# An FFN on split fp32 weights: high parts first, wide casts, and one early feature group of three blocks by seven products

## The chip, the cores and the metric

The kernel runs on one core of a Trainium2 chip. The metric is the device time of one launch in microseconds. Five queues work side by side: TensorE (PE in the profile; its weight loads are PEld), VectorE (DVE), ScalarE (ACT), GpSimd (POOL) and SyncE (SP), which here issues nearly all DMAs. Weights (about 300 MB of fp32) stream from HBM once.

## The reference

One transformer layer on 256 latent tokens of 2048 features, with 256 context tokens that serve as keys and values only. The second half, which the change touches, is an adaLN-modulated SwiGLU FFN of 5632 hidden features:

```python
def swiglu(u, w_gate, w_up, w_down):
    return (jax.nn.silu(u @ w_gate) * (u @ w_up)) @ w_down
...
x = layer_norm(DN_ALPHA * x + g1 * (heads @ w_out[layer]), ln1_g[layer], ln1_b[layer])

x = layer_norm(DN_ALPHA * x + g2 * swiglu(modulate(x, sh2, sc2), w_gate[layer], w_up[layer], w_down[layer]),
               ln2_g[layer], ln2_b[layer])
```

`sh2`, `sc2` and `g2` are columns of `silu(c) @ w_ada + b_ada`, one row each.

## The kernel before

**Split products.** Each fp32 operand is split into a high part, a cast to fp32r on ScalarE, and a low part, the difference on VectorE. A product is three matmuls of 128x128 by 128x512 (`mm3`, L340): high x high, high tokens x low weights, low tokens x high weights, in this order for each chunk of 128 features. A weight load brings 4 chunks x 512 columns (1 MB, `load_raw`) into one of four raw buffers; `split_raw` (L320) cuts it into two pieces of 1024 columns, each with its own cast (L331) and difference (L332), in one of four slots of `hi` and `lo`. Such a step ("a plain step", `project`, L1494) makes 4 chunks x 2 token halves x 3 = 24 matmuls.

**Stages.** Up to about 390 us an order searched by a planner (`Flow`) runs modulation, q/k/v, attention and the output projection; its steps take slots of `hi` and `lo` as the pool gives them. The FFN that follows is written as lists of steps, and the framework's scheduler sets the order on each queue from that. Gate and up have 11 blocks of 512 hidden features; the 2048 input features are four groups of four chunks.

- *Early projections* (about 390 to 582 us). Features of groups 2 and 3 need `sh2` and `sc2`, which are still being summed from `w_ada`: VectorE multiplies and adds 1024 columns at a time (`vector_sum`, L466), 32 times for two groups, then turns the row into columns (`folded_columns`, L1150) with a few matmuls. Meanwhile TensorE works on the groups that are ready: group 0 for blocks 0 to 2, groups 0 and 1 for blocks 3 to 9 (`first_half`, L1655), with results copied by ScalarE to `spills` in SBUF. `merge` (L290) spreads the ada steps evenly between the projection steps (L1713). The last two projections run after the last features are there.
- *Late gate and up* (about 582 to 878 us). Block pairs (f0, f0 + 1): group 2 of the gate goes through `folded` (L1541), Winograd's form of Strassen's scheme: with two token halves, two halves of four chunks and two column blocks, seven products take the place of eight. VectorE forms differences of weights and (once) of tokens for it, ScalarE copies partial sums from bank to bank. Plain steps of up run between the products. Then gating, a transpose through DRAM (`flip_steps`, L1610) and the split of the hidden features (`place`).
- *Down* (about 878 to 1110 us). `down_step` for four column blocks, with group `FOLD_H` again folded, the sums for `g2` beside it, and the last normalisation at the end.

PSUM has four `acc` and four `wk` banks. SyncE issues loads in order, so a load that waits for a raw buffer holds those behind it.

Of the kernel before, what the change touches and what calls it, by code (L numbers as in the profile page):

```python
# [13 lines left out]
F32 = mybir.dt.float32  # L14
# [9 lines left out]
P = 128  # L24
# [26 lines left out]
FOLD_K = 8  # L51
FOLD_H = 6
# [19 lines left out]
class Flow:  # L72
# [194 lines left out]
def dit_layer(ctx: ExitStack, tc: tile.TileContext, x, c, cx, c_ctx, w_ada, b_ada, w_in, q_norm_g,  # L267
# [8 lines left out]
    whl = ctx.enter_context(tc.tile_pool(name="whl", bufs=HL_BUFS))  # L276
# [17 lines left out]

    def fill(pool, nbytes):

        pool.tile([P, nbytes // 4], F32, tag="fill", name="fill")
# [5 lines left out]
    stats = main.tile([P, NT, 4, 6], F32, tag="stats", name="stats")  # L303

# [12 lines left out]
    def load_split(w, k0, c0, nk=G4, width=NB, spare=False):  # L317
        return split_raw(load_raw(w, k0, nk, c0, width), spare)

    def split_raw(raw, spare=False):  # L320

        parts = []
        for s in range(0, raw.shape[-1], SUB * NB):
            n = min(SUB * NB, raw.shape[-1] - s)
# [3 lines left out]
            else:  # L328
                hi = whl.tile([P, SUB * NB], F32R, tag="hi", name="hi")
                lo = whl.tile([P, SUB * NB], F32R, tag="lo", name="lo")  # L330
            nc.scalar.copy(hi[:, :n], raw[:, s : s + n])  # L331
            nc.vector.tensor_tensor(lo[:, :n], raw[:, s : s + n], hi[:, :n].bitcast(F32), op=ALU.subtract)  # L332
            parts += [(hi[:, j : j + NB], lo[:, j : j + NB]) for j in range(0, n, NB)]
        return parts
# [138 lines left out]
    def split_rows(sb, dst, s):  # L473
        hi = whl.tile([P, SUB * NB], F32R, tag="hi", name="hi")[:, :NB]
        lo = whl.tile([P, SUB * NB], F32R, tag="lo", name="lo")[:, :NB]
# [112 lines left out]
    def flow_weights(w, k0, nk, c0, width=NB, where=("raw", "araw"), spare=False, small=False, behind=(None, None)):  # L588
# [3 lines left out]
        for s in range(0, nk * width, SUB * NB):  # L592
# [4 lines left out]
            def cast(hl=hl, s=s, n=n):  # L597
                if spare:
                    hl.hi, hl.lo = (b4([P, SUB * NB], F32R, c) for c in ("hi", "lo"))
                else:  # L600
                    hl.hi = whl.tile([P, SUB * NB], F32R, tag="hi", name="hi")
                    hl.lo = whl.tile([P, SUB * NB], F32R, tag="lo", name="lo")
# [547 lines left out]
    def folded_columns(sb, n):  # L1150
# [7 lines left out]
        ps = wk_bank()  # L1158
        for q in range(4):
            nc.tensor.matmul(ps[32 * q : 32 * q + 32, :n], lhsT=grp[0], rhs=rv[:, q], start=True, stop=True)  # L1160
        return ps

    def second_modulation(g, sums):
        def done(sb):
            ps = folded_columns(sb, 8)
# [820 lines left out]
```

## Time and profile before

| | us |
|---|---|
| time, median of 3 runs (lowest to highest) | 1122.85 (1122.63 to 1124.99) |
| span of the profiled execution | 1121.0 |
| first FFN matmul | 390.4 |
| last matmul ends about | 1110 |
| granted TensorE clock, mean | 0.996 |

The span runs from the first to the last instruction of one profiled execution; no time of that execution beside its span is recorded, and the runs' median lies 1.85 us above it. In the timeline each matmul of 512 columns lasts 0.39 us, yet consecutive ones overlap: what counts is the distance from start to start. In the groups, a row has busy time, the mean length of one in ns, then the idle time of the engine just before and what ended it.

### The profile page before, as it was taken

To read this page: it belongs to the slowest core of one execution; us is meant where nothing else is said; L and a number is where in the kernel's file an instruction comes from. 1 tells how busy PE (TensorE), PEld (TensorE's weight loads), DVE (VectorE), ACT (ScalarE), POOL (GpSimd) and SP (SyncE) were. 2 spreads that over 40 slices of the span, in tenths; PEclk is the share of its full clock that TensorE was granted. 3 is DMA by queue.
4 is the path that set the end of the run, shared out by engine and by line. 5 is a ranking of instruction groups with operands and counts; after the bars stand their busy time and mean duration, and the time that the engine had idled before them with its cause. 6 is when DMAs were issued, how large, how long until landed. Compare 5 with 4: busy or idle time off the path is not lost.

```text
span 1121.0 us, 14130 instructions
## 1 busy us (share of the span) xinstructions
PE 1102.3 (98%) x5213; PEld 883.7 (79%) x5213; DVE 903.4 (81%) x1133; ACT 598.7 (53%) x875; POOL 36.7 (3%) x82
## 2 busy tenths in 40 slices
PE   8999999999999999999999999999999999999995
PEld 6766688777887788888888878888888888888884
DVE  5763589899999888787778697988996987689876
ACT  3341554878685356444475565767766344444442
POOL 1000030110100001000000000000000000000000
PEclk9999999999999999999999999999999999999998
DMA  9999999778999778999956677777776998669742
GB/s 321 394 385 375 393 362 377 247 234 274 345 332 395 249 269 321 348 318 296 336 182 216 223 220 266 234 246 271 228 267 216 329 348 293 228 235 379 287 149 76
DMA packets 178317, 321.26 MB, mean 287 GB/s; under 512 B 8732, under 2 KB 43196, under 8 KB 175943
## 3 DMA queue, kind: packets, MB, share of 16 engines
q1 hardware_dynamic: 177528, 320.03, 81.7%
q8 instruction: 41, 0.67, 0.2%
q10 hardware_dynamic: 720, 0.33, 0.1%
q14 instruction: 28, 0.23, 0.1%
HBM read 304.07 MB, written 16.25 MB: 286 GB/s over the span
## 4 chain that ended last, share of the span: by engine, by line
PE 91%; DMA 3%; DVE 2%; ACT 1%; SPq 1%; issue 0%; ACTq 0%; DVEq 0%
PE acc L341 20%; PE acc L343 20%; PE acc L342 20%; PE wk L342 8%; PE wk L341 8%; PE wk L343 8%; PE wk L1081 2%; PE wk L654 2%; DMA raw<-in_w_in_dram 2%; DVE lo L332 1%; DMA lgb<-in_ln_g_dram 1%; PE wk L755 1%; SPq L569 1%; DMA xt<-in_x_dram 0%; PE wk L1414 0%
## 5 line engine op out<-in xcount | busy, mean ns | idle before, releaser
L331 ACT CAST hi<-raw 128x1024 fp32r<-128x1024 f32 x279 | 290.7, 1054 | 256.4 <-PE acc L343 162.4
L332 DVE TENSOR_TENSOR lo<-raw,hi 128x1024 fp32r<-128x1024 f32 x279 | 336.1, 1220 | 103.6 <-ACT hi L331 101.4
L341 PE MATMUL acc<-hi,u2h 128*128 128x512 f32 x390 | 152.5, 391 | 0.0
L343 PE MATMUL acc<-hi,u2l 128*128 128x512 f32 x390 | 151.7, 390 | 0.7 <-DVE u2l L1669 0.7
L342 PE MATMUL acc<-lo,u2h 128*128 128x512 f32 x390 | 151.8, 389 | 0.0
L603 ACT CAST hi<-raw 128x1024 fp32r<-128x1024 f32 (+1 forms) x86 | 87.4, 1030 | 113.8 <-DMA raw<-in_w_in_dram 63.2
L466 DVE SCALAR_TENSOR_TENSOR adav<-raw,cs,adav 128x512 f32<-128x512 f32 (+1 forms) x128 | 121.4, 949 | 8.4 <-DMA raw<-in_w_ada_dram 4.9
L606 DVE TENSOR_TENSOR lo<-raw,hi 128x1024 fp32r<-128x1024 f32 (+1 forms) x86 | 101.3, 1194 | 16.3 <-ACT hi L603 15.5
L341 PE MATMUL acc<-hi,uh 128*128 128x512 f32 x256 | 103.7, 405 | 1.3 <-ACT uh L769 0.8
L342 PE MATMUL wk<-lo,u2h 128*128 128x512 f32 x264 | 103.1, 390 | 0.5 <-DVE lo L332 0.5
L343 PE MATMUL wk<-hi,u2l 128*128 128x512 f32 x264 | 102.7, 389 | 0.0
L341 PE MATMUL wk<-hi,u2h 128*128 128x512 f32 x264 | 102.2, 389 | 0.0
L342 PE MATMUL acc<-lo,uh 128*128 128x512 f32 x256 | 100.5, 392 | 0.6 <-DVE lo L606 0.6
L343 PE MATMUL acc<-hi,ul 128*128 128x512 f32 x256 | 100.1, 391 | 0.4 <-DVE ul L784 0.4
L341 PE MATMUL acc<-hi,hTh 128*128 128x512 f32 x236 | 92.0, 390 | 0.4 <-ACT acc L1901 0.4
L342 PE MATMUL acc<-lo,hTh 128*128 128x512 f32 x236 | 91.8, 389 | 0.0
L343 PE MATMUL acc<-hi,hTl 128*128 128x512 f32 x236 | 91.8, 389 | 0.0
L343 PEld LDWEIGHTS acc<-hi,u2l 128*128 128x128 f32 x390 | 73.2, 188 | 16.2 <-DVE u2l L1669 1.1
L341 PEld LDWEIGHTS acc<-hi,u2h 128*128 128x128 f32 x390 | 73.2, 188 | 16.1 <-ACT u2h L1668 0.8
L342 PEld LDWEIGHTS acc<-lo,u2h 128*128 128x128 f32 x390 | 73.2, 188 | 15.1
L341 PEld LDWEIGHTS acc<-hi,uh 128*128 128x128 f32 x256 | 48.1, 188 | 19.0 <-issue 5.6
L342 PEld LDWEIGHTS wk<-lo,u2h 128*128 128x128 f32 x264 | 49.5, 188 | 12.0 <-DVE lo L332 1.8
(277 smaller groups left out, 1748.0 us busy)
## 6 DMA issues: line engine op xcount, KB each, us to landing
raw<-in_w_ada_dram SPq DMA_DIRECT2D x70, 1024.0 KB, 7.7
raw<-in_w_gate_dram SPq DMA_DIRECT2D x44, 1024.0 KB, 6.7
raw<-in_w_up_dram SPq DMA_DIRECT2D x44, 1024.0 KB, 5.6
raw<-in_w_down_dram SPq DMA_DIRECT2D x44, 1024.0 KB, 5.8
raw<-in_w_ada_dram SPq DMA_DIRECT2D x48, 512.0 KB, 5.9
raw<-in_w_in_dram SPq DMA_DIRECT2D x18, 1024.0 KB, 11.0
raw<-in_w_out_dram SPq DMA_DIRECT2D x16, 1024.0 KB, 6.5
pd<-hx SPq DMA_DIRECT2D x64, 128.0 KB, 3.4
```

Of the source, the lines that this page charges most:

```text
L331: nc.scalar.copy(hi[:, :n], raw[:, s : s + n])
L332: nc.vector.tensor_tensor(lo[:, :n], raw[:, s : s + n], hi[:, :n].bitcast(F32), op=ALU.subtract)
L341: nc.tensor.matmul(ps, lhsT=xh, rhs=w[0], start=first, stop=False, skip_group_check=seeded)
L342: nc.tensor.matmul(ps, lhsT=xh, rhs=w[1], start=False, stop=False, skip_group_check=seeded)
L343: nc.tensor.matmul(ps, lhsT=xl, rhs=w[0], start=False, stop=last, skip_group_check=seeded)
L466: nc.vector.scalar_tensor_tensor(a[:, c : c + piece], raw[:, f : f + piece], cs[:, 4 * (g * (G4 * NB // w) + j) + 2, None], a[:, c : c + p ...
L569: nc.sync.dma_start(room.t, w[k0 * P : (k0 + 1) * P, c0 : c0 + width])
L603: nc.scalar.copy(hl.hi[:, :n], raw.t[:, s : s + n])
L606: nc.vector.tensor_tensor(hl.lo[:, :n], raw.t[:, s : s + n], hl.hi[:, :n].bitcast(F32), op=ALU.subtract)
L654: nc.tensor.matmul(bank.t[32 * j : 32 * j + 32, :width], lhsT=cs[:, 4 * k + 2 - 2 * i : 4 * k + 34 - 2 * i], rhs=raw.t[:, c * width : (c + ...
L755: nc.tensor.transpose(ps.t[:, (j * 2 + t) * P : (j * 2 + t + 1) * P], src, ident)
L1081: nc.tensor.matmul(o_ps.t[:, : 2 * P].rearrange("p (g q) -> p g q", q=32), lhsT=v, rhs=pv[:, k], start=k == 0, stop=k == 3)
```

## The change

1. *Seven products early.* `EARLY_F = (4, 6, 8)`: group 1 (features 512 to 1023, `FOLD_E = 4`) of these blocks no longer takes a plain step each for gate and up. `folded` runs with the gate columns and the up columns of the same block as its pair, after token forms made once (`token_forms(*heads, ...)`). Its five stages stand between plain steps of other blocks; then group 0 of up and of gate is added onto the same banks, and the results go to `spills` (up by VectorE additions, gate by ScalarE copies). The gate weights land in two tiles of their own (`halves_of`), the up weights in a raw buffer.
2. *High parts first.* `products` issues, for all chunks and token halves of a step, the two matmuls on the high weights, then those on the low weights. The attention part, the first FFN products and the tail keep `mm3`.
3. *Wide casts.* `hi` and `lo` are one tile each with four slots of 1024 columns, given in turn (`part_pair`); a plain step's 2048 columns are cast and subtracted by one instruction each, in two neighbouring slots, the first of them even. The last steps (`fine=True`) keep pieces of 1024. The planner's part takes the slot that its own schedule shows free first.
4. *Smaller ones.* The ada steps are spread by a count of VectorE work (`spread`); the matmuls behind `folded_columns` are a step of their own; some VectorE operations of the late stage go over both token halves at once; the `g2` sums run over 1024 columns.

```diff
-        for s, s.start, pools in self.search()[0]:
+        best = self.search()[0]
+        free = [(0.0, i) for i in range(self.room["hl"])]
+        left = {b: b.left for s, _, _ in best for b in s.give}
+        for s, s.start, pools in best:
             for b, b.pool in zip(s.take, pools):
-                pass
+                if b.pool == "hl":
+                    free.sort()
+                    b.slot = free.pop(0)[1]
...
+    def spread(steps, extra, load):
+
+        loads = [load.get(s, (24, 2)) for s in steps]
+        share = (sum(v for _, v in loads) + 2 * len(extra)) / sum(n for n, _ in loads)
+        res, extra, debt = [], list(extra), 0.0
+        for s, (n, v) in zip(steps, loads):
+            res.append(s)
+            debt += n * share - v
+            while extra and debt > 0:
+                res.append(extra.pop(0))
+                debt -= 2
+        return res + extra
...
+    def part_pair(n):
+
+
+        wide = SUB * NB
+        if n > wide:
+            turns[0] += turns[0] % 2
+        i = turns[0] % HL_BUFS
+        turns[0] += -(-n // wide)
+        return [parts[c].rearrange("p b n -> p (b n)")[:, i * wide : i * wide + n] for c in ("hi", "lo")]
...
+    def split_raw(raw, spare=False, fine=False):
+
+        n = raw.shape[-1]
+        cols = []
+        for s in range(0, n, SUB * NB if spare or fine else n):
+            m = SUB * NB if spare or fine else n
...
+                hi, lo = part_pair(m)
+            split(hi, lo, raw[:, s : s + m])
+            cols += [(hi[:, j : j + NB], lo[:, j : j + NB]) for j in range(0, m, NB)]
+        return cols
...
+    def products(banks, w, first, last, seeded=False):
+
+
+        for j, x in enumerate(banks):
+            for i, (ps, xs) in enumerate(x):
+                for h in xs:
+                    nc.tensor.matmul(ps, lhsT=h, rhs=w[j][0], start=first and not seeded and j == 0 and h is xs[0], stop=False,
+                                     skip_group_check=seeded)
+        for j, x in enumerate(banks):
+            for ps, xs in x:
+                nc.tensor.matmul(ps, lhsT=xs[0], rhs=w[j][1], start=False, stop=last and j == len(banks) - 1,
+                                 skip_group_check=seeded)
...
+    def halves_of(w, k0, c0):
+
+        res = []
+        for i, c in enumerate("hl"):
+            half = halves0.pop(0) if halves0 else pb.tile([P, 2 * NB], F32, tag=f"hT{c}0", name="half")
...
-    def folded(columns, forms, shared):
+    def folded(columns, forms, shared, first=wk_bank):
...
+        def product(ps, m, piece, first):
+            products([[(ps, forms[m][j])] for j in range(2)], split_raw(piece), first, True, not first)
...
+    def fold_steps(f):
...
+        def shared(e):
+            nc.scalar.copy(up[:, 0, :], e)
+
+        def stage(i):
+            if i == 0:
+                st["it"] = folded([(w, FOLD_E, f * NB) for w in (w_gate, w_up)], early, shared, acc_bank)
+            st["banks"] = next(st["it"])
+
+        def own(i, w):
+            project(st["banks"][i], w, f, 0, None, 3, True)
+            for t in reversed(range(NT)):
+                if i:
+                    nc.vector.tensor_add(up[:, t, :], up[:, 0, :], st["banks"][i][t])
+                else:
+                    nc.scalar.copy(gate[:, t, :], st["banks"][i][t])
...
+        steps = fold_steps(f)
+        load.update(zip(steps, ((6, 2), (6, 3), (12, 3), (12, 2), (6, 1), (24, 3), (24, 2))))
+        normal = [s for e in range(f) if e not in EARLY_F for s in firsts_of[e]]
+        at = len(normal) - 2
+        rest, AT_F = first_half[at:], at
+        mixed = []
+        for s in steps[:4]:
+            mixed += [s, rest.pop(0)]
...
-    run(merge(first_half[2 * ONE_F + 1 : cutoff], side))
+    run(spread(first_half[2 * ONE_F + 1 : cutoff], side, load))
```

More of the change, by code (lines that the diff above doesn't have):

```diff
@@ L51 @@
 FOLD_K = 8
+FOLD_E = 4
+EARLY_F = (4, 6, 8,)
 FOLD_H = 6
@@ L600, in cast @@
                 else:
[L601 to L602 removed]
+                    hl.hi, hl.lo = (parts[c][:, hl.slot, :] for c in ("hi", "lo"))
                 nc.scalar.copy(hl.hi[:, :n], raw.t[:, s : s + n])
@@ L1157, in folded_columns, with sums, place @@
         rv = r[:, : 4 * n].rearrange("p (c q) -> p q c", q=4)
[L1158 to L1161, printed above, removed]
+        def sums():
+            ps = wk_bank()
+            for q in range(4):
+                nc.tensor.matmul(ps[32 * q : 32 * q + 32, :n], lhsT=grp[0], rhs=rv[:, q], start=True, stop=True)
+            return ps
+        return sums
     def second_modulation(g, sums):
+        st = {}
         def done(sb):
-            ps = folded_columns(sb, 8)
+            st["sums"] = folded_columns(sb, 8)
+        def place():
+            ps = st["sums"]()
             ks = slice(g * 4, g * 4 + 4)
@@ L1169, in done @@
             combine(g)
-        return ada_vector_steps((3 * D + g * NB, 4 * D + g * NB), NB, sums, done)
+        return ada_vector_steps((3 * D + g * NB, 4 * D + g * NB), NB, sums, done) + [place]
     def flow_vector(starts, width, a, span):
@@ L1558, in folded @@
         yield
-        products(e, 1, b11, True)
+        product(e, 1, b11, True)
         tt(b12, b22, b12, op=ALU.subtract)
@@ L1562, in folded @@
         yield
-        products(b, 2, b11, False)
+        product(b, 2, b11, False)
         c = acc_bank()
@@ L1630, in places @@
         def places():
-            for t in range(NT):
-                place(f, t, hf[t])
+            place(f, wide)
             if f == FOLD_H:
@@ L1648, in step @@
                 if g == 0:
-                    st["accs"] = [acc_bank() for _ in range(NT)]
+                    st["accs"] = [acc_bank() if f < ONE_F else wk_bank() for _ in range(NT)]
                 project(st["accs"], w_, f, g, 0, groups[f] * 4 - 1)
@@ L1653, in step @@
                         nc.scalar.copy(spills[f][i][:, t, :], st["accs"][t])
-            first_half += [lambda g=g, step=step: step(g) for g in range(groups[f])]
+            firsts_of[f] += [lambda g=g, step=step: step(g) for g in range(groups[f])]
+    def fold_steps(f):
+        st = {}
+        gate, up = spills[f]
+        def shared(e):
[11 more added lines that the diff above has]
+                    nc.scalar.copy(gate[:, t, :], st["banks"][i][t])
+        return [lambda i=i: stage(i) for i in range(5)] + [lambda: own(1, w_up), lambda: own(0, w_gate)]
+    first_half, load = [], {}
+    for f in range(SPLIT_F):
+        if f not in EARLY_F:
+            first_half += firsts_of[f]
+    AT_F = 0
+    for f in reversed(EARLY_F):
+        steps = fold_steps(f)
[6 more added lines that the diff above has]
+            mixed += [s, rest.pop(0)]
+        if f + 1 < SPLIT_F and len(rest) > 2:
+            first_half[at:] = mixed + [steps[4]] + steps[5:] + rest
+        else:
+            first_half[at:] = mixed + steps[4:] + rest
     late_sums = [lambda: vector_sums(2 * NB), lambda: pb.tile([P, 2 * NB], F32, tag="lgb", name="adav")]
```

148 lines of the change are left out of this document (76 added, 72 removed).

## The prediction

> **What bounds the kernel now.** I read the page first (shares, chain of waits), then windows over the FFN, then single matmuls in the timeline.
>
> ```profile
> span 1121.0 us, 14130 instructions
> ...
> PE 1102.3 (98%) x5213; PEld 883.7 (79%) x5213; DVE 903.4 (81%) x1133; ACT 598.7 (53%) x875; POOL 36.7 (3%) x82
> ...
> PE 91%; DMA 3%; DVE 2%; ACT 1%; SPq 1%; issue 0%; ACTq 0%; DVEq 0%
> ```
>
> TensorE is busy 98% of the span and makes 91% of the chain that ended last. A busy PE need not be at its pace, so the timeline is needed: two rows of one unbroken run of projections, the first and the last of 123.
>
> ```profile
> 469.78 0.39 PE L341 MATMUL acc<-hi,u2h 128*128 128x512 f32 x1
> ...
> 497.43 0.39 PE L343 MATMUL acc<-hi,u2l 128*128 128x512 f32 x1
> ```
>
> (497.43 − 469.78) / 122 = 0.2266 us from start to start. That is the price of one matmul wherever nothing is late. [...]
>
> The windows show what the other engines do meanwhile: first the stretch the change rewrites (early projections, 434 to 571 us), then the late gate and up stage.
>
> ```profile
> 434.00:571.00 137.00, 137.00 (x627) 112.98 (x626) 100.45 (x92) 68.19 (x81) 1.64 (x7) 1.00 0.92 314
> ```
> ```profile
> 571.00:878.00 307.00, 306.46 (x1350) 252.80 (x1350) 259.84 (x289) 193.56 (x244) 0.00 (x0) 1.00 0.72 237
> ```
>
> Columns after the width are PE, PEld, DVE, ACT, POOL, then clock, DMA share and GB/s. In the early stretch PE never idles, DVE is busy 100.45 of 137 us (73%), DMA has a share of 0.92. Late, DVE is at 259.84 / 307 = 85%. So TensorE's count of matmuls sets the FFN's time, and VectorE is next. Where VectorE was late it shows as three places in the late stage:
>
> ```profile
> 645.77 0.39 PE L341 MATMUL wk<-hi,u2h 128*128 128x512 f32 x1
> 646.32 0.50 PE L342 MATMUL wk<-lo,u2h 128*128 128x512 f32 x1 [0.17 <-DVE lo L332]
> ...
> 653.04 0.39 PE L341 MATMUL wk<-hi,u2h 128*128 128x512 f32 x1
> 653.80 0.50 PE L342 MATMUL wk<-lo,u2h 128*128 128x512 f32 x1 [0.37 <-DVE lo L332]
> 654.14 0.40 PE L343 MATMUL wk<-hi,u2l 128*128 128x512 f32 x1
> ```
> ```profile
> 668.66 0.39 PE L341 MATMUL wk<-hi,u2h 128*128 128x512 f32 x1
> 669.01 0.50 PE L342 MATMUL wk<-lo,u2h 128*128 128x512 f32 x1
> 669.35 0.39 PE L343 MATMUL wk<-hi,u2l 128*128 128x512 f32 x1
> ```
> ```profile
> 636.00:670.00 34.00, 33.46 (x145) 26.79 (x144) 32.02 (x38) 19.90 (x26) 0.00 (x0) 1.00 0.61 192
> ```
>
> The low part of a weight piece arrived late. The steps are 0.55, 0.76 and 0.35 us instead of 0.23 (0.32 + 0.53 + 0.12 lost), and the step behind each is 0.34 instead of 0.23: together 1.3 us.
>
> **The change, part by part.** *Seven products.* A block's group 1 (features 512 to 1023) costs gate and up 2 x 24 = 48 matmuls; seven products of 6 cost 42. Three blocks: 18 matmuls x 0.2266 = **4.1 us** less on TensorE. Everything else of the fold lies on ScalarE, VectorE and DMA and costs only what makes a matmul late. The prices there:
>
> ```profile
> L332 DVE TENSOR_TENSOR lo<-raw,hi 128x1024 fp32r<-128x1024 f32 x49 | 59.7, 1220 | 29.4 <-ACT hi L331 29.3
> L466 DVE SCALAR_TENSOR_TENSOR adav<-raw,cs,adav 128x1024 f32<-128x1024 f32 x29 | 37.2, 1282 | 3.3 <-DMA raw<-in_w_ada_dram 3.2
> L1155 DVE STREAM_TRANSPOSE flip<-adav 128x512 f32<-128x512 f32 x4 | 2.8, 707 | 0.1
> L1156 DVE TENSOR_REDUCE fold<-flip 128x16 f32<-128x512 f32 x4 | 2.7, 676 | 0.0
> ```
> ```profile
> L1560 DVE TENSOR_TENSOR raw<-raw 128x1024 f32<-128x1024 f32 x7 | 8.4, 1203 | 0.0
> L1891 DVE TENSOR_TENSOR raw<-raw,room 128x2048 f32<-128x2048 f32 x3 | 6.9, 2287 | 0.1
> L1753 DVE TENSOR_TENSOR spill<-spill,wk 128x512 f32<-128x512 f32 x4 | 2.6, 680 | 0.0
> ```
> ```profile
> 517.29 1.28 DVE L466 SCALAR_TENSOR_TENSOR adav<-raw,cs,adav 128x1024 f32<-128x1024 f32 x1
> 518.49 1.22 DVE L332 TENSOR_TENSOR lo<-raw,hi 128x1024 fp32r<-128x1024 f32 x1
> 519.62 1.28 DVE L466 SCALAR_TENSOR_TENSOR adav<-raw,cs,adav 128x1024 f32<-128x1024 f32 x1
> ```
>
> Back to back a sum takes 1.20 us and a low part 1.13 us from start to start, 0.08 to 0.09 less than they last. The new order runs from the second gate step of block 3 to the gate step that ends block 8. TensorE: 24 + 3 x (42 products + 4 x 24 plain steps between them + 2 x 24 for group 0) = 582 matmuls = 131.9 us (600 and 136.0 before). VectorE in the same steps, back to back: 19 whole low parts x 2.20 (2.287 − 0.09) = 41.8; 21 product pieces x 1.13 = 23.7; 12 weight differences x 1.13 = 13.6; 6 additions of up x 0.60 = 3.6; the token forms about 2.6 (six operations of 256 or 512 columns); 32 sums x 1.20 = 38.4; their columns 4 x 0.65 + 4 x 0.60 = 5.0. Sum **128.7 us**; with the isolated durations (2.287, 1.220, 1.203, 0.680, 1.282) it is 138. So VectorE goes from 73% to 98% of the stretch. If it still waits 3.2 us for ada weights, as now, it stands at 131.9, exactly TensorE's time. The loss this brings is shown by no row of the stretch; bounds: 0 (the low part is asked for later, next item) and 138 + 3.2 − 131.9 = 9.3 us, less some 3 us by which VectorE can lag at the ends (an estimate: about half of a step of 24 x 0.2266 at each), so 6. Nearest is the window above with VectorE at 32.02 of 34 us (94%): 1.3 us lost, which over 132 us would be 5. There the low part was wanted by the second matmul; now most plain steps give it 16. I take **2 us**.
>
> *High parts first.* `products` issues a step's high matmuls (16 of 24) and then the 8 low ones: the low part is due 16 x 0.2266 = 3.6 us after the step begins, not 0.23. In a single product it is 4 of 6, 0.9 us. The same number of matmuls, the same number of weight loads. All three delays above are under 0.9 us, so I take them as gone: **−1.3 us** (bounds 0 and −1.3). Nothing else in the FFN waits for a low part for long, so no more is to be had.
>
> *Wide casts.* Each pair of 1024-column casts and differences becomes one of 2048.
>
> ```profile
> L331 ACT CAST hi<-raw 128x1024 fp32r<-128x1024 f32 x49 | 51.6, 1054 | 54.8 <-PE acc L343 52.3 <-DMA raw<-in_w_up_dram 1.3 <-DVE adav L466 1.2
> L1653 ACT COPY spill<-acc 128x512 f32<-128x512 f32 x26 | 15.3, 589 | 14.0 <-PE acc L343 12.8
> ...
> L1480 ACT CAST u2h<-uf 128x512 fp32r<-128x512 f32 x2 | 1.2, 622 | 0.0
> ```
>
> ScalarE now waits for slots, 52.3 us of it on TensorE, so what it saves is idle time and counts nothing; on VectorE a pair costs 2.287 instead of 2.44, already in the sum. But a wide cast needs two of four slots free at once, and starts the step's first matmul only when all 2048 columns are done: some 1054 + 1024 x 0.84 = 1.9 us, 0.84 being (1054 − 622 of a 512 cast) / 512. With one-slot products between plain steps, an odd slot is skipped and the plain step always returns to the same two. Then its cast may begin when the last step's high matmuls end (8 x 0.2266 = 1.8 us before that step does), and must end one product later (1.4 us): 3.2 − 1.9 − about 0.2 of signals = **1.1 us to spare**. A single copy of 0.59 us ahead of it in ScalarE's queue fits; two do not. I cost it at 0; cover gone, it is rival 2.
>
> *Smaller edits.* Merged multiplies, additions and places of the late stage take little off VectorE: about 30 wide pairs x 0.15 = 4.6 of 260 us, and PE is at pace there: 0. The sums of the gate rows in 1024 columns: VectorE off the path: 0. `place` as a step of its own moves eight 8-column matmuls behind VectorE's columns: within 0.1. Fixed slots in the attention part keep the planner's order: 0, within 0.5 either way. The tail keeps 1024-column pieces and its order: 0.
>
> **Sum.** −4.1 − 1.3 + 2.0 = −3.4 us: the span would be 1117.6. The median of the runs, 1122.85, lies 1.85 above the profiled span; the same on top gives **1119.5 us**.
>
> **Rivals.** *1. VectorE becomes the bound.* For it: the 98% above; the additional product pieces and differences stand in one queue with the ada sums, so a late sum delays the next low part. Against: 0.9 to 3.6 us of new patience. By the isolated durations the loss is 6 us: −4.1 − 1.3 + 6 = +0.6, so 1123.5, no change. [...]
>
> *2. Plain steps' wide slots and raw buffers (slower).* The one mechanism: in the pattern product, plain step, product, the next wide cast starts later than 1.1 us after the slot comes free, because ScalarE is in a copy or because the raw weights have not landed. For it:
>
> ```profile
> SPq L311 <- DVE lo L332: 35.9, 18, 5.1
> SPq L456 <- DVE lo L332: 32.0, 7, 6.2
> SPq L456 <- DVE adav L466: 26.1, 7, 5.0
> ```
>
> These are waits of the weight loads (SyncE's queue) for VectorE to release a raw buffer. The fold keeps one of the four raw buffers for the up columns over three plain steps, and a full VectorE releases the others later. There are 12 such plain steps early, about 20 in the late pairs, some 6 with the down pairs; at 0.25 us each, 38 cost 9.5 us: −5.4 + 2 + 9.5 = +6, 1129; at a third of it, 1123. It decides from about 0.15 us a step on (5.7 us) that the kernel is slower. Against: ScalarE is half idle.
>
> *3. VectorE keeps up.* Loss 0: −5.4 us, 1117.5.
>
> **How the numbers follow.** Forecast 0.48 (own range 1118 to 1120.8), rival 3 0.14, rival 1 0.22 (1120.8 to 1125), rival 2 0.16 (above 1123; two thirds of it above 1125.1). About 0.2%, 2.2 us, is what a measurement of this kernel can tell from no change: under 1120.6 is faster, over 1125.1 slower. Faster: 0.43 of the forecast's 0.48 and rival 3: 0.57. Slower: 0.11 of rival 2 and 0.04 of rival 1 = 0.15. Same: 0.28. The range leaves out the worst of rival 2 and the very edge of rival 3: 1116.5 to 1126.
>
> **What would show it.** Matmul records fewer by about 18, with starts 0.2266 us apart. Right: in the early stretch VectorE at 95% or more, gaps of matmuls before low parts summing to about 2 us; no gap at the three late places. Rival 1: low parts late at most folds, 5 us or more. Rival 2: matmuls on high parts waiting for ScalarE or for raw DMA, also in the late stage. The forecast is wrong from the ground up if the start-to-start time itself changes with the new order of matmuls, or if the part before 390 us moves by more than 0.5 us.

## The result and the profile after

The changed kernel takes 1128.89 us (median of 5 runs, 1128.35 to 1130.66) against 1122.63 us for the kernel before, measured beside it (5 runs, 1121.07 to 1124.99): a ratio of 1.0057 (95% interval 1.0043 to 1.0071). It is slower by some 6 us. The forecast was 1119.5 us, with a range of 1116.5 to 1126, and 15% on slower. The profile below is of the run of 1130.23 us (mean granted clock 0.995); the three runs at 0.996 took 1128.35 to 1128.89.

The page of the changed kernel, in the lines that answer to those shown of before:

```profile
span 1128.4 us, 13825 instructions
...
PE 1101.1 (98%) x5195; PEld 880.2 (78%) x5195; DVE 913.0 (81%) x1000; ACT 592.3 (52%) x781; POOL 46.7 (4%) x80
...
PE 89%; DMA 4%; ACT 3%; DVE 2%; issue 1%; SPq 0%; ACTq 0%; DVEq 0%
```

TensorE did lose 18 matmuls (5213 to 5195), and still the span grew by 7.4 us. What is new in the chain of work is ScalarE: 1% before, 3% now.

The windows of the changed kernel over the early projections, a short stretch in them, the late stage and the down stage (columns as in the prediction, clock third from the end):

```profile
434.00:575.00 141.00, 136.87 (x609) 111.34 (x607) 129.15 (x106) 75.69 (x78) 7.84 (x4) 0.99 0.84 298
438.70:442.10 3.40, 3.40 (x10) 2.63 (x9) 3.40 (x5) 0.00 (x0) 0.00 (x0) 0.50 0.20 48
575.00:878.00 303.00, 303.00 (x1352) 250.96 (x1350) 249.53 (x208) 185.21 (x192) 2.52 (x3) 1.00 0.71 235
885.00:1110.00 225.00, 222.50 (x976) 182.51 (x975) 170.28 (x130) 90.01 (x70) 0.95 (x1) 1.00 0.73 264
```

The same three long windows of the kernel before:

```profile
434.00:575.00 141.00, 141.00 (x644) 116.29 (x643) 102.75 (x97) 72.19 (x89) 1.64 (x7) 1.00 0.89 305
...
575.00:878.00 303.00, 302.46 (x1332) 249.49 (x1332) 257.55 (x285) 189.56 (x236) 0.00 (x0) 1.00 0.73 240
885.00:1110.00 225.00, 224.60 (x988) 184.71 (x986) 179.22 (x195) 95.06 (x108) 1.58 (x3) 1.00 0.72 260
```

In the late stage TensorE is never idle after the change. The losses lie in the early stretch (4.1 of 141 us idle, and 3.4 us at half the granted clock) and in the down stage (2.5 of 225 us idle). VectorE, which I feared most, stands at 129.15 of 141 us (92%).

The table cuts the profiled execution of each kernel into stages, by starts of matmuls in the trace: up to the first FFN matmul; early projections up to the transposes of the last features; late gate and up; down. Beside them are the medians of the runs and the ratio to the kernel before, measured beside each. Labels are those of the experiments below.

| | up to FFN | early | late | down | time | ratio (95%) |
|---|---|---|---|---|---|---|
| before | 390.4 | 178.8 | 307.3 | 231.7 | 1122.63 | |
| before, a second look (e8) | 392.6 | 178.9 | 306.0 | 231.4 | 1123.8 (one run) | |
| **after** | 392.5 | **182.5** | 306.2 | **234.4** | 1128.89 | 1.0057 (1.0043–1.0071) |
| e1 no early products | 392.6 | 180.6 | 306.5 | 234.4 | 1126.32 | 1.0033 (1.0020–1.0046) |
| e2 narrow casts | 392.3 | 178.7 | 306.1 | 231.5 | 1123.68 | 1.0008 (0.9998–1.0018) |
| e3 old order | 390.0 | 214.6 | 416.5 | 256.1 | 1296.28 | 1.1539 (1.1507–1.1571) |
| e4 = e1 + e2 | 389.1 | 180.4 | 306.3 | 231.5 | 1123.31 | 1.0006 (0.9996–1.0017) |
| e5 = e2, slots from the pool | 390.2 | 178.6 | 306.2 | 231.5 | 1122.62 | 0.9998 (0.9986–1.0009) |
| e6 = e5, one step moved | 391.2 | 180.2 | 306.2 | 231.5 | 1123.30 | 1.0012 (1.0002–1.0022) |
| e7 before, slots in turn | 390.9 | 179.5 | 305.9 | 231.3 | 1123.06 | 1.0012 (1.0001–1.0023) |
| e9 = e5, two blocks | 392.2 | 180.8 | 306.1 | 231.5 | 1124.42 | 1.0009 (0.9999–1.0019) |
| e10 = e5, old order | 390.9 | 179.9 | 307.9 | 233.7 | 1126.11 | 1.0035 (1.0024–1.0046) |
| e11 = e5, short sums | 391.3 | 176.5 | 306.1 | 231.6 | 1120.08 | 0.9979 (0.9967–0.9990) |
| e13 casts halved, slots as after | 392.3 | 182.5 | 306.1 | 231.6 | 1126.10 | 1.0027 (1.0013–1.0041) |
| e14 high first alone, acc banks | 391.5 | 179.0 | 305.9 | 231.5 | 1122.31 | 0.9997 (0.9986–1.0008) |
| e15 three blocks, new spread | 391.6 | 180.9 | 306.2 | 231.5 | 1123.65 | 1.0006 (0.9995–1.0017) |
| e16 two blocks, new spread | 393.1 | 177.5 | 306.2 | 231.6 | 1121.41 | 0.9988 (0.9978–0.9997) |
| e17 two blocks, old spread | 390.8 | 182.4 | 306.2 | 231.5 | 1124.68 | 1.0019 (1.0009–1.0028) |
| e18 three blocks, as e16 | 390.5 | 180.2 | 306.1 | 231.6 | 1123.10 | 1.0003 (0.9992–1.0014) |
| e19 as e16, more delay | 391.7 | 178.0 | 306.2 | 231.6 | 1121.09 | 0.9984 (0.9974–0.9993) |

The first row against the second is the measure for the rest: the same program differs by 2.2 us before the FFN and by 1.3 us in the late stage from one execution to the next, but by 0.3 us or less in the early and down stages. Four of the profiles (after, e13, e17, e18) have a stretch at half clock in the early stage, which adds 1.5 to 1.7 us there. The last features' transposes themselves, about 2 us, are in no column. So a difference of a microsecond is read from early and down, and not from the whole span. The 2.2 us that the changed kernel's profile shows before the FFN are inside this spread.

Four places in the changed kernel show the losses. First, the transposes of group 1 (tile `xt`, L1526), in the timeline (start, length, then the row; in brackets the engine's idle time and who ended it):

```profile
434.47 1.04 PE L1526 MATMUL wk<-ident,xt 128*128 128x128 f32 x8
...
435.16 1.48 ACT L1531 ACTIVATE uf<-wk,mB,mA 128x256 f32<-128x256 f32 x3 [1.26 <-PE wk L1526]
...
436.52 0.62 ACT L1533 CAST u2h<-uf 128x512 fp32r<-128x512 f32 x1
...
437.20 0.72 PE L379 MATMUL wk<-hi,u2h 128*128 128x512 f32 x2 [1.70 <-ACT u2h L1533]
...
440.26 0.63 PE L379 MATMUL wk<-hi,u2h 128*128 128x512 f32 x1
...
440.69 0.63 PE L379 MATMUL wk<-hi,u2l 128*128 128x512 f32 x1
```

TensorE has nothing behind the transposes that it can do without group 1, so it waits for ScalarE to modulate and cast it: 1.70 us. Then it runs 3.4 us at half clock, where matmuls start 0.43 us apart (440.69 − 440.26) instead of 0.2266: 1.5 us more. Second, a plain step behind a product, in the same view:

```profile
453.11 0.59 ACT L1738 COPY spill<-wk 128x512 f32<-128x512 f32 x1 [4.59 <-PE wk L383]
453.60 1.90 ACT L370 CAST hi<-raw 128x2048 fp32r<-128x2048 f32 x1
...
455.55 0.19 PEld L379 LDWEIGHTS wk<-hi,u2h 128*128 128x128 f32 x1 [1.77 <-ACT hi L370]
```

ScalarE stood 4.59 us in a copy that waits for TensorE's last matmul on that bank; the cast for TensorE's next step stands behind it in the same queue, so it starts when TensorE runs out of work, and lasts 1.90 us. The same order of copy and cast stands at 488.32 us and costs 1.0 us. Third, the first wide cast of the FFN leaves TensorE idle for 0.64 us:

```profile
406.71 0.50 PE L379 MATMUL acc<-hi,u2h 128*128 128x512 f32 x1 [0.64 <-ACT hi L370]
```

Fourth, the down stage, where the longest wait is for a low part:

```profile
1052.17 1.91 ACT L370 CAST hi<-raw 128x2048 fp32r<-128x2048 f32 x1 [8.11 <-PE acc L379]
```
```profile
1063.05 1.28 DVE L1254 BATCH_NORM_STATS2 stats<-xt 128x6 f32<-128x512 f32 x2
...
1064.25 3.48 DVE L371 TENSOR_TENSOR lo<-raw,hi 128x1024 fp32r<-128x1024 f32 x3
...
1065.51 0.50 PE L388 MATMUL acc<-lo,hTh 128*128 128x512 f32 x1 [1.50 <-DVE lo L371]
```

ScalarE stood idle for 8.11 us before the wide cast, until TensorE released its slots; the casts behind it came later, and by then the operations of the last normalisation stood ahead of the next three low parts on VectorE.

### The profile page after: what moved, and what is told of

It is laid out like the page before. It is cut to its first block, busy times and chain, and to the rows that moved or that the text cites. A ratio compares the mean times of both kernels' runs of the same rounds, so it can differ in the third digit from the quotient of the medians.

```text
span 1128.4 us, 13825 instructions
## 1 busy us (share of the span) xinstructions
PE 1101.1 (98%) x5195; PEld 880.2 (78%) x5195; DVE 913.0 (81%) x1000; ACT 592.3 (52%) x781; POOL 46.7 (4%) x80
## 4 chain that ended last, share of the span: by engine, by line
PE 89%; DMA 4%; ACT 3%; DVE 2%; issue 1%; SPq 0%; ACTq 0%; DVEq 0%
PE wk L379 20%; PE acc L379 17%; PE wk L383 10%; PE acc L387 9%; PE acc L389 9%; PE acc L388 8%; PE acc L383 8%; DMA raw<-in_w_in_dram 2%; PE wk L1125 2%; PE wk L698 2%; ACT hi L370 1%; DMA raw<-in_w_out_dram 1%; DVE lo L371 1%; DMA pd<-hx 1%; PE wk L387 1%
## 5 line engine op out<-in xcount | busy, mean ns | idle before, releaser
L370 ACT CAST hi<-raw 128x2048 fp32r<-128x2048 f32 (+1 forms) x173 | 267.6, 1553 | 275.7 <-PE acc L379 96.0
L371 DVE TENSOR_TENSOR lo<-raw,hi 128x2048 fp32r<-128x2048 f32 (+1 forms) x173 | 314.6, 1835 | 92.3 <-ACT hi L370 83.8
L379 PE MATMUL wk<-hi,u2h 128*128 128x512 f32 x398 | 156.2, 393 | 3.9 <-ACT hi L370 2.2
L379 PE MATMUL wk<-hi,u2l 128*128 128x512 f32 x398 | 155.7, 392 | 0.0
L512 DVE SCALAR_TENSOR_TENSOR adav<-raw,cs,adav 128x1024 f32<-128x1024 f32 (+1 forms) x96 | 114.3, 1191 | 11.0 <-DMA raw<-in_w_ada_dram 8.7
L379 PE MATMUL acc<-hi,u2h 128*128 128x512 f32 x234 | 91.2, 390 | 0.6 <-ACT hi L370 0.6
L379 PEld LDWEIGHTS wk<-hi,u2h 128*128 128x128 f32 x398 | 75.2, 189 | 20.8 <-ACT hi L370 3.0
L379 PE MATMUL acc<-hi,u2l 128*128 128x512 f32 x234 | 91.1, 389 | 0.0
L379 PEld LDWEIGHTS wk<-hi,u2l 128*128 128x128 f32 x398 | 75.2, 189 | 15.9 <-DVE u2l L1534 0.3
L383 PE MATMUL acc<-lo,u2h 128*128 128x512 f32 x234 | 64.7, 390 | 0.3 <-DVE lo L371 0.3
```

Source lines behind the costliest of these rows:

```text
L379: nc.tensor.matmul(ps, lhsT=h, rhs=w[j][0], start=first and not seeded and j == 0 and h is xs[0], stop=False, skip_group_check=seeded)
L383: nc.tensor.matmul(ps, lhsT=xs[0], rhs=w[j][1], start=False, stop=last and j == len(banks) - 1, skip_group_check=seeded)
L512: nc.vector.scalar_tensor_tensor(a[:, c : c + piece], raw[:, f : f + piece], cs[:, 4 * (g * (G4 * NB // w) + j) + 2, None], a[:, c : c + p ...
```

## The experiments

Theory A: the wide casts cost the time, since they need two slots at once (the second rival). Theory B: VectorE is full early and eats what the seven products save (the first rival). Theory C, in the later runs: behind the transposes of group 1 TensorE's queue holds nothing that needs group 0 alone. Diffs are against the changed kernel unless another is named.

**e1 to e4: one part undone at a time.** e1 takes the early products out, e2 the wide casts, e4 both; e3 puts the order of `mm3` back.

```diff
# e1
-EARLY_F = (4, 6, 8,)
+EARLY_F = ()
...
-    first_half[AT_F + 1 : AT_F + 1] = [lambda: early.update(token_forms(*heads, FOLD_E, homes))]
# e2
-        for s in range(0, n, SUB * NB if spare or fine else n):
-            m = SUB * NB if spare or fine else n
+        for s in range(0, n, SUB * NB):
+            m = min(SUB * NB, n - s)
# e3, in products
-                for h in xs:
-                    nc.tensor.matmul(ps, lhsT=h, rhs=w[j][0], ...
...
+                mm3(ps, *xs, w[j], first and not seeded and j == 0, last and j == len(banks) - 1, seeded)
```

> The changed kernel with the seven early products undone (blocks 4, 6 and 8 take their plain steps for features 512 to 1023 again); wide casts, the fixed turn of slots and high parts first stay. Theory A (wide casts in a fixed turn of four slots keep TensorE waiting for the high cast): part of the loss stays, the wait near 406 us and the four in the down stage, so 1123 to 1125 us. Theory B (the early products overload VectorE and nothing else costs): the early stage goes back to 179 us and the time falls to 1121 to 1122 us.

> The changed kernel with casts and differences of 1024 columns, one slot each in turn; the early products and high parts first stay. Theory A: the waits for a high cast go, near 406, 437, 455 and 491 us and in the down stage; 1118 to 1121 us. Theory B: VectorE has 0.15 us more per pair to do, so the early waits stay or grow; 1127 to 1130 us.

> The changed kernel with the old order of matmuls within a step (high, low, high for each chunk and token half), wide casts and early products kept. If high parts first is what makes the low part's lateness bearable: waits for low parts at nearly every product, 1132 to 1140 us, and the late stage, 306.2 us with the change, at 308 us or more. If the order does not matter: 1128 to 1130 us.

> The changed kernel without the early products and with casts of 1024 columns: what is left is high parts first, the fixed turn of slots and the small edits. Theory A: only the gain of the late stage is left, 1121 to 1122 us. If the fixed turn of slots by itself costs: 1123 us or more.

Measured: e1 1126.32, e2 1123.68, e4 1123.31 us. Neither theory's numbers came out: e1 is slower than both said, and e2 lies between them. Wide against narrow casts is 5.2 us with the products (1128.89 − 1123.68) and 3.0 us without (1126.32 − 1123.31). With narrow casts the early products make the kernel 0.4 us longer (1123.68 − 1123.31), which is nothing within the intervals of about 1 us, although TensorE has 18 matmuls less. (Their early stretches, one profile each, stand the other way, 178.7 against 180.4, so a gain of a microsecond is not excluded.) Of the wide casts' cost, 2.9 us lie in the down stage, with and without the products (234.4 against 231.5). The early stretch pays only with the products: 3.8 us (182.5 against 178.7), 1.5 of them the half clock, against 0.2 without (180.6 against 180.4). e3 was far beyond every expectation: 1296.28 us. Its waits, by group (us in total, times, longest):

```profile
PE wk L381 <- ACT hi L370: 42.7, 40, 1.8
PE wk L382 <- DVE lo L371: 31.9, 28, 2.8
PE acc L381 <- ACT hi L370: 23.0, 32, 1.7
```

In the old order all chunks of a step use high and low weights alike up to its end, so both slots of a wide pair come free only when the step is over. The next cast (1.92 us in the mean in the changed kernel) and difference (2.29 us) then stand open: TensorE waits 72 times for ScalarE, 0.9 us in the mean and up to 1.8, and 31 times for low parts, up to 2.8. High parts first is what makes wide casts bearable.

**e7 and e8: the kernel before, with slots in turn, and as it is.** e7 gives the kernel before the changed kernel's slots (the planner's by its schedule, later ones in a fixed turn), with 1024-column casts; e8 is the kernel before, unchanged, for a second profile.

```diff
+    parts = {c: whl.tile([P, HL_BUFS, SUB * NB], F32R, tag=c, name=c) for c in ("hi", "lo")}
+    turns = [0]
...
-                hi = whl.tile([P, SUB * NB], F32R, tag="hi", name="hi")
-                lo = whl.tile([P, SUB * NB], F32R, tag="lo", name="lo")
+                hi, lo = part_pair()
```

> The kernel before with one thing changed: slots of hi and lo are given by the planner's schedule up to the FFN, and in fixed turn in the FFN, casts of 1024 columns as before. If the fixed slots cost in the part before the FFN: that part at 392 us against 390.4 and the time 1 to 3 us longer. If not: 1122 to 1123 us, with the FFN within 0.5 us.

> The kernel before, unchanged, for a second profile: how far the part before the FFN (390.4 us in the first profile) moves from one execution to the next. If it moves by about 2 us: what the changed kernel shows there (392.5 us) says nothing. If it stays within 0.5 us: the change costs there too.

e7 is 0.12% slower than before (1.0012, 1.0001 to 1.0023): 0.7 us by the medians, barely more than nothing. The waits of TensorE in the late stage of the kernel before were, in the profile that I predicted from:

```profile
PE wk L342 <- DVE lo L332: 0.5, 2, 0.4
```

In e8's profile, the same program, no such row is left, and the late stage takes 306.0 us. The delays that I meant to save are not in every execution.

**e5, e6, e13: slots, one step's place, and the width alone.** e5 has narrow casts and takes slots from the pool; e6 also moves the up step of block 3, group 0, to where the kernel before had it; e13 keeps the paired slots of the changed kernel, but fills them by two instructions of 1024 columns.

```diff
# e5, in part_pair, with narrow casts as in e2
-        i = turns[0] % HL_BUFS
...
+        return [whl.tile([P, SUB * NB], F32R, tag=c, name=c)[:, :n] for c in ("hi", "lo")]
# e6, after e5
+    i0, i1 = 2 * ONE_F + 1, AT_F + 2
+    first_half[i0 : i1 + 1] = [first_half[i1]] + first_half[i0:i1]
# e13
-            split(hi, lo, raw[:, s : s + m])
+            for c in range(0, m, SUB * NB):
+                split(*(x[:, c : min(m, c + SUB * NB)] for x in (hi, lo, raw[:, s : s + m])))
```

> The changed kernel with casts of 1024 columns and with the slots of hi and lo taken from the pool again, in the planned part and in the FFN (no fixed turn); early products, high parts first and the small edits stay. Theory A (the fixed turn of slots is a part of the cost beside the wide casts): the part before the FFN returns to 390.4 us, the waits at 406 and 437 us shrink, 1119 to 1121 us. Rival (the turn costs nothing, what is left early is the order of steps): as with narrow casts in fixed turn, 1123 to 1124 us.

> As the kernel before this one, with one step moved: the first up step of block 3, which needs group 0 alone, runs ahead of the second gate step of block 3 and of the first early product, which both need the tokens of group 1 that are just being made; the gate of block 3 takes acc banks so that banks suffice. Theory C (the wait of 1.9 us near 437 us is TensorE with nothing left that needs group 0 alone): that wait goes, 1.5 to 2.4 us less than the kernel before this one. If it is only slots: the same time.

> The changed kernel with its slots as they are (a plain step takes two neighbouring ones, the first even, in fixed turn), but cast and subtracted in pieces of 1024 columns. Theory A1 (it is the turn of slots: an odd slot skipped, the plain step always in the same two): as slow as the changed kernel, 1127 to 1129 us, the down stage at 234.4 us. Theory A2 (it is the wide instruction, which starts only when both slots are free and lets the first matmul go only when all 2048 columns are done): as with narrow casts in single slots, 1123 to 1124 us, the down stage at 231.5 us.

e13 tells the two halves of the wide casts apart. The down stage is back at 231.6 us: there the instruction over 2048 columns costs, since each half can no longer start when one slot is free. In e13 the casts of that place come one by one, the first at 1049.45, and more of the low parts get onto VectorE ahead of the normalisation:

```profile
1049.45 1.05 ACT L371 CAST hi<-raw 128x1024 fp32r<-128x1024 f32 x1 [2.01 <-issue]
1051.28 1.05 ACT L371 CAST hi<-raw 128x1024 fp32r<-128x1024 f32 x1 [0.77 <-PE acc L380]
```
```profile
1052.18 3.50 DVE L372 TENSOR_TENSOR lo<-raw,hi 128x1024 fp32r<-128x1024 f32 x3 [3.94 <-issue]
```

The early stretch stays at 182.5 us in e13, with a half-clock stretch like the changed kernel's, so there it is not the width of the instruction alone. But e13 waits in other places: beside the transposes 0.7 us each for two low parts and a copy, 0.5 and 0.3 for casts, and none of 1.3 for a cast. How the paired slots bring these about is not shown. The time, 1126.10, lies between the two expectations. With slots from the pool (e5) the stretch is 178.6, and the kernel is level with before, not faster as theory A had it. Its waits up to 575 us (beside the 0.7 us for `u2l` that the kernel before has too):

```profile
PE wk L369 <- ACT u2h L1523: 1.7, 1, 1.7
PE acc L373 <- DVE lo L361: 1.3, 1, 1.3
PE wk L369 <- DVE u2l L1524: 0.2, 1, 0.2
```

From start to start, over the pace, they are 1.74, 1.44 and 0.37 us: 3.6 in all, about half of it for VectorE. e6 removed the wait at the transposes and got others, of 2.19 and 1.79 us (steps from start to start, over the pace), for ScalarE's casts: no gain.

**e9, e10, e11: less to do for VectorE.** e9 folds two blocks instead of three; e10 has the old order with narrow casts; e11 multiplies and adds 64 of 1024 columns in the early ada sums, so that most columns of the shift and scale of features 1024 to 2047 are left unsummed.

```diff
# e9, after e5
-EARLY_F = (4, 6, 8,)
+EARLY_F = (6, 8,)
# e10, after e5: products as in e3
# e11, after e5
-                vector_sum(raw, st["a"], w, g, i)
+                vector_sum(raw, st["a"], w, g, i, 64 if ns == 2 else None)
```

> Early products for blocks 6 and 8 alone, casts of 1024 columns, slots from the pool, high parts first. TensorE saves 12 matmuls, 2.7 us, VectorE has 10 us less to add, and no product stands right behind the tokens of group 1. Theories B and C both: waits fall from 3.8 us to 1 or 2, the early stage 177 to 178 us, 1120.5 to 1122 us. If each product block costs what it saves, whatever its place: 1122 to 1123 us.

> Early products with casts of 1024 columns and slots from the pool, but the old order of matmuls in a step (high, low, high). If high parts first is what carries a full VectorE: waits for low parts at most products of the early stretch, that stage at 181 us or more against 178.6, 1125 to 1128 us. If narrow casts alone are enough: 1122 to 1123 us.

> Early products with casts of 1024 columns and slots from the pool; each of the 32 ada sums of the early stretch works on 64 of its 1024 columns, so the shift and scale of features 1024 to 2047 are left mostly unsummed; all loads and steps stay. This takes some 30 us off VectorE in that stretch. Theory B (a full VectorE makes the early waits): the wait of 1.4 us near 484 us goes, 177 us or less for the stage, 1120 to 1121 us. Theory C (the order of steps): the wait of 1.9 us near 434 us stays whatever VectorE has to do, and the stage stays above 176 us; without any wait it would be 174.8.

e11 is the only kernel in which three blocks gain more than half of what they save: 176.5 us early, 0.9979 of before. All that is left there, beside the `u2l` wait of before, is the wait at the transposes; the window from 434 us on has VectorE at 106.10 us:

```profile
434.00:575.00 141.00, 140.04 (x637) 115.41 (x638) 106.10 (x134) 87.25 (x111) 4.73 (x7) 1.00 0.85 302
```

This came out as theories B and C both had it: the 2.1 us that the early stretch gains on e5 are about what e5 waits for VectorE (1.44 + 0.37). But VectorE is not the whole: e9 has a third of the folds' work less there and no wait for a weight's low part, and its early stretch is longer than in e5 (180.8 against 178.6 us), with waits for casts of 2.1 us in all and the 1.7 at the transposes. Its time, 1124.42, lies above all that was expected of it. e10's median is 3.5 us over e5's; its profile is longer in the early (+1.3), late (+1.7) and down (+2.1) stages.

**e14 to e19: places in the queues against a full VectorE.** All have narrow casts and slots from the pool. e14 has no early products, and all early projections on `acc` banks. e15 has e6's order; its ada steps are spread by their own cost and start later. e16 folds two blocks, with blocks 3 and 4 on `acc` banks and such a spread; e17 is e16 with the changed kernel's spread; e18 is e16 with three blocks; e19 is e16 with twice the delay.

```diff
# e14
-                    st["accs"] = [acc_bank() if f < ONE_F else wk_bank() for _ in range(NT)]
+                    st["accs"] = [acc_bank() if True else wk_bank() for _ in range(NT)]
# e16 (e17 without the spread; e18 with EARLY_F = (4, 6, 8); e15 and e19 with 4 for 2)
-EARLY_F = (4, 6, 8,)
+EARLY_F = (6, 8)
...
-        share = (sum(v for _, v in loads) + 2 * len(extra)) / sum(n for n, _ in loads)
-        res, extra, debt = [], list(extra), 0.0
+        cost = [0 if i % 9 == 8 else 5 if i % 9 == 7 else 2 for i in range(len(extra))]
+        share = (sum(v for _, v in loads) + sum(cost) + 2) / sum(n for n, _ in loads)
+        res, extra, debt = [], list(extra), -2.0
...
-                debt -= 2
+                debt -= cost.pop(0)
...
+                    st["accs"] = [acc_bank() if f < 5 else wk_bank() for _ in range(NT)]
```

> High parts first and the small edits alone: no early seven products, casts in 1024 columns, slots from the pool as before, and all early projections on the four acc banks. The run with narrow casts and the fixed turn, without the fold, waited 0.9 us behind the transposes of group 1 and lost a little in other places. If the banks cause that wait, it goes: 178.2 to 178.8 us between the first FFN matmul and the last features, 306 late, 231.5 down, and the time is 1121.5 to 1122.5. If the order of the steps causes it, the wait stays and the time is 1122.5 to 1123.5. In both cases high parts first alone gains nothing that can be told from before (my forecast had -1.3).

> Seven products for three blocks, casts in 1024 columns, slots from the pool, the up step of block 3 ahead of the products; new is that the ada sums are spread by what each step costs VectorE (2 for a sum, 5 for the step that turns the row into columns) and start 4 units late. If VectorE's clustering is what delays the low parts of the products, the two waits of about 1.8 to 2.2 us shrink below 1 each: 176 to 178 us early, 1119.5 to 1121. If VectorE is simply full (95% and more), the same time is lost in other places: 179 to 180 us, 1122.5 to 1124.

> Seven products for two blocks (6 and 8), casts in 1024 columns, slots from the pool, blocks 3 and 4 on acc banks, the ada sums spread by cost with 2 units' delay. 12 matmuls fewer are 2.7 us; VectorE has about 7 us more room than with three blocks. If waits come from a full VectorE, they fall below 1 us in all and the time is 1120 to 1121.3. If they come from where the sums and the turned rows stand in VectorE's queue, they stay near 2 to 3 us: 1122 to 1124.

> The same as the run with two blocks and sums spread by cost, but with the spread of the changed kernel (every ada step counted 2). If the places of the sums decide, this one is slower than that by 0.5 to 1.5 us (1121.5 to 1123.5); if not, the two are within 0.5 us.

> The best version with two blocks so far (blocks 6 and 8; 1121.41 us, 177.5 us early) with block 4 as a third one; nothing else changes. One block more is 6 matmuls less, 1.4 us on TensorE, and 3.3 to 3.5 us more net work for VectorE in a stretch that it already fills to 89%. If only the places of the sums matter: 176 to 176.5 us early and 1119.8 to 1120.5. If a third block fills VectorE, the low parts come late again: 178.5 to 181 us early and 1122.5 to 1124, as in the run with three blocks and sums spread by cost.

> The same best version with two blocks, but with 4 units of delay for the sums instead of 2. If the gain of that run over the one with the old spread (3.3 us) came from sums that follow later, this is as fast or a little faster: 1120.5 to 1121.5. If it hangs on the particular order that the scheduler then makes around the transposes of group 1, the wait of 1.9 us can come back: 1122.5 to 1124.

e16 and e17 have the same matmuls, banks and VectorE instructions, and their early stretches differ by 4.9 us (177.5 and 182.4), of which 1.6 are the half clock in e17's profile. The medians differ by 3.3 us, more than the 0.5 to 1.5 expected. Their windows, e16's first:

```profile
434.00:575.00 141.00, 139.56 (x641) 114.95 (x640) 125.14 (x122) 79.95 (x102) 5.80 (x7) 1.00 0.86 305
```
```profile
434.00:575.00 141.00, 138.38 (x620) 113.17 (x620) 122.16 (x118) 77.39 (x96) 5.51 (x6) 0.99 0.84 296
```

VectorE is busier in the quicker one. What differs is the order in the queues. TensorE's waits up to 575 us in e17:

```profile
PE wk L369 <- ACT hi L360: 2.1, 2, 1.6
PE acc L369 <- ACT u2h L1523: 1.7, 1, 1.7
PE acc L379 <- DVE u2l L1776: 0.7, 1, 0.7
```

And in e18, with three blocks:

```profile
PE acc L370 <- ACT u2h L1524: 1.7, 1, 1.7
PE wk L370 <- ACT hi L361: 1.6, 1, 1.6
PE acc L380 <- DVE u2l L1777: 0.7, 1, 0.7
```

A wait like the last row of each is in the kernel before too (0.7 us for `u2l`). The other two kinds are the ones shown above of the changed kernel, and neither is a wait for VectorE, which e18 has busy 131.0 of 141 us. So e18's time is the one expected of a full VectorE, and its waits are not; the same holds of e15. The wait at the transposes is gone in e14, e16 and e19. In e19 one sees why: behind the transposes TensorE's queue holds eight matmuls whose features are there already, before it asks for group 1:

```profile
432.64 1.04 PE L1517 MATMUL wk<-ident,xt 128*128 128x128 f32 x8
...
433.43 0.48 PE L370 MATMUL acc<-hi,u2h 128*128 128x512 f32 x1
...
434.70 0.62 ACT L1524 CAST u2h<-uf 128x512 fp32r<-128x512 f32 x1
...
435.38 0.53 PEld L370 LDWEIGHTS acc<-hi,u2h 128*128 128x128 f32 x3 [0.28 <-ACT u2h L1524]
```

The banks alone don't bring this about: e17 and e18 have e16's banks, and the wait. Nor does a step moved by hand: e15 has e6's order and no such wait, but 4.4 us of waits for ScalarE's casts, and is at 1.0006. The other kind, in e19's ScalarE rows (its one wait that is left):

```profile
525.25 1.08 ACT L1742 COPY spill<-acc 128x512 f32<-128x512 f32 x2 [6.83 <-PE acc L374]
526.83 0.57 ACT L1619 COPY acc<-acc 128x512 f32<-128x512 f32 x1 [0.51 <-PE acc L374]
527.32 1.99 ACT L361 CAST hi<-raw 128x1024 fp32r<-128x1024 f32 x2
```

ScalarE is idle 6.83 us in front of a copy that waits for TensorE, then copies a product's partial sum, which again waits for TensorE's last matmul; only then come the casts for the plain step behind that product, which TensorE needs at once. Its matmul starts at 528.42, 1.62 us late. ScalarE has time (80 of 141 us busy); its order has not. In these rows the cast, whose weights had landed by 524.40, does not pass the copy: it starts at 527.32, as the copy ends.

**The best version.** e16 and e19 (1121.41 and 1121.09 us; 0.9988, 0.9978 to 0.9997, and 0.9984, 0.9974 to 0.9993) beat the kernel before by a little over 0.1% and the changed one by over 7 us. Their gain is what twelve matmuls save (12 x 0.2266 = 2.7 us) less one wait of 1.4 to 1.8 us.

## Why the prediction was wrong, step by step

- **Wide casts, "I cost it at 0": the step that failed.** They cost 5.2 us (after against e2). Without them the kernel is level with before (e2, 1.0008), which is not yet the 3.4 us of gain that was forecast; the next items have the rest. The 1.1 us to spare were worked out for a pattern in which the paired slots come free at a step's high matmuls and nothing but one copy stands ahead in ScalarE's queue (of the 0.2 us of signals in it, the kernel before has as much on the way to the cast: at 473.38 one starts 0.43 us after the start, at 472.95, of the matmul that releases it, 0.20 over the pace; at 406.71 after the change a matmul starts 0.05 us after its cast ends). The rows show two things that I had left out: the copy ahead waits itself for TensorE (4.59 us at 453.11), so the cast starts when the work is already gone; and at the down stage's end the cast starts only when both slots are free (ScalarE idle for 8.11 us before it), which puts the low parts behind the normalisation. e13 and e1 place 2.9 us of it in the down stage, by the instruction's width. The early part of it (182.5 against 178.7 in e2, or 2.3 us without the half clock of that execution) is there only beside the seven products, and e13, with paired slots and narrow instructions, has as much; as its waits lie elsewhere, the early mechanism is read from the changed kernel's rows and not proved by a run.
- **Rival 2 (slower, 1129) named the mechanism**, a wide cast that starts late because ScalarE is in a copy, and its time came out, but by luck. Its count did not: I spread 0.25 us over 38 steps, 20 of them in the late pairs. The late pairs lose nothing (TensorE 303.00 of 303), and the cost sits in a few waits of 0.2 to 1.7 us. Raw buffers play no part in the waits shown. I gave it 0.16, on the ground that ScalarE is half idle. An idle share says nothing of a queue whose head waits for the very engine that waits for its tail.
- **Seven products, −4.1 us.** Right for TensorE: 18 matmuls less at the old pace. The loss put against them, 2 us by VectorE, left out the waits for ScalarE. With narrow casts the products gain nothing that the medians show (e2 against e4, e5 against e14). In e5 the loss is 1.8 us for VectorE's low parts, close to the 2 taken, and 1.7 us for ScalarE at the transposes, for which the prediction had no term; the early stretches of e5 and e14 agree with it (−4.1 + 3.6 = −0.5; 178.6 against 179.0). In the changed kernel's early stretch low parts of weights cost 0.4 us and waits for ScalarE 5.0, of which 3.3 are for wide casts.
- **Rival 1 (VectorE the bound)** fell as a bound: e16 against e17, and e18 with VectorE at 93% and no wait for a weight's low part. As a part of the loss it stands: e5's 1.8 us, which are gone in e11. Shorter sums also change every place in the queues, so e11 doesn't prove that VectorE's time was the cause. (By the isolated durations that the prediction names, VectorE's sum is about 137 us, not 138, and the loss at most 5, not 6.) What exactly makes the framework's scheduler choose the one order or the other was not found.
- **VectorE at 98%** was counted a little high: from 437.2 us, where the new order begins, to 573.0 it is busy 125.9 of 135.8 us (93%), where 128.7 of 131.9 were added up.
- **High parts first, −1.3 us.** The delays are gone, and nothing was gained: e14, which has this and the smaller edits alone, is at 0.9997 (0.9986 to 1.0008), and the kernel before in another execution has no such delays either. I had taken one execution's accident for a property. The order matters all the same, as cover: without it e10 loses 3.5 us (to e5) and e3 167 us (to the changed kernel).
- **Smaller edits, 0, and slots in turn, within 0.5.** e14 agrees for the edits (1122.31 against 1122.57 us beside it). The slots in turn cost rather more: 0.7 us in e7, whose interval is 0.1 to 2.6, and 1.1 us in e2 against e5.
- **"The part before 390 us moves by more than 0.5 us"** as a sign against the forecast was no good sign: the same program moves by 2.2 us there.

The sum, with what was measured in place of what I took: −4.1 for the products and +4.5 for their waits (e2 stands 0.4 above e4), +5.2 for the wide casts, and +0.7 for all that e4 has (1123.31 against 1122.61 beside it; its interval holds 0) make +6.3, as measured (1128.89 − 1122.63). That they add up is no check, since the +4.5 is what is left over. The forecast's −3.4 is missed by 9.7 us: 5.2 by the wide casts, 2.5 by the products' waits, 1.3 by the delays that were not to be saved, 0.7 by the rest. The steps are differences of medians, each uncertain by about 1 us.

## What to carry to other kernels

An engine that is half idle can still be the one that is late (ScalarE, busy 75.69 of 141 us, left TensorE waiting for 3.9 us of them): look at what stands ahead of the needed instruction in its queue, and whether that head waits for the engine which you mean to feed. Joining two instructions into one saved 0.15 us of 2.44 on VectorE and some 0.2 us of 2.11 on ScalarE here, but it tied two buffers together, which cost 2.9 us in the down stage, and the gain counts for nothing if the engine had time. Before a microsecond of waits is taken for a saving, look at a second profile of the same program.

## What was not expected of the hardware

After a wait of 1.70 us TensorE ran at half its clock for a while. Besides e3, nine profiles have TensorE wait 1.7 us behind the transposes of group 1. In four of them (the changed kernel, e13, e17, e18; mean granted clock 0.995) a stretch at a granted clock of 0.50 follows; in the other five (e2, e5, e9, e10, e11; 0.996 to 0.997) none does. In the changed kernel it lasts 3.413 us, from 438.66 us, 1.46 us after the wait is over, and matmuls start 0.427 us apart in it. It costs 1.5 to 1.7 us, as much as the wait itself. e3, with its many waits, has a mean granted clock of 0.965, and 0.93 from 575 to 878 us:

```profile
575.00:878.00 303.00, 260.33 (x1025) 198.75 (x1025) 188.52 (x155) 137.46 (x142) 0.55 (x3) 0.93 0.55 184
```

The stretches of unchanged clock in the changed kernel's trace, from 5.17 to 1121.33 us, are 433.493, 3.413 and 679.252 us long, and the one at full clock in the trace of the kernel before is 1105.918 us: 127, 1, 199 and 324 times 3.4133 us. What decides whether a wait is followed by half clock is not shown: the same 1.7 us are in four profiles and not in five, and in the changed kernel no half clock follows the waits of 1.34 us at 455.55 and 1.50 us at 1065.51.
